# A hybrid attention trunk on one core: the opening's first loads on two queues, x's first column rounded by VectorE, and the lambda scalars moved behind the first projection pair

## The chip, the cores and the metric

The kernel runs on one core of one Trainium2 chip. The core has five engines with queues of their own: TensorE (PE in the profile, PEld for its weight loads), VectorE (DVE), ScalarE (ACT), GpSimd (POOL) and SyncE (SP), and 16 DMA engines that serve the transfers which SP, ACT and POOL issue. The metric is the device time in microseconds (us), as the median over runs.

## The reference

Two layers are applied to x, 256 tokens of 2048 features, all in float32:

```python
for l in range(2):
    h = rms_norm(x, pre_mix_norm[l])
    proj = h @ w_in[l]                     # 2048 -> 6144: q, k, v of both groups
    o_sb = stick_breaking(q_sb, k_sb, v_sb)          # 8 heads of 128
    lam = exp(sum(lq1*lk1)) - exp(sum(lq2*lk2)) + lam_init
    o_d = (softmax(q1 k1) - lam * softmax(q2 k2)) v_d  # 8 heads
    o_d = rms_norm(o_d, diff_subln) * (1 - lam_init)
    x = x + rms_norm(concat(rms_norm(o_sb), o_d) @ w_o[l], post_mix_norm[l])
    h = rms_norm(x, pre_ffn_norm[l])
    f = (silu(h @ w_gate[l]) * (h @ w_up[l])) @ w_down[l]   # 2048 -> 5632 -> 2048
    x = x + rms_norm(f, post_ffn_norm[l])
```

`lam` is one number for each layer. It comes from four vectors of 64 numbers and is used only when the second softmax is subtracted from the first. The weights are 411 MB in float32.

## The kernel before, in words

**Numbers in two parts.** A float32 product on TensorE is made of three products of rounded parts. Each weight tile `raw` (128 x 1024, two chunks of 128 rows by 512 columns) is split by ScalarE into `hi`, its rounded value (line 286), and by VectorE into `lo`, the rest (line 289). The activations are split in the same way (`xT`, lines 802 and 803). TensorE then adds hi x hi, hi x lo and lo x hi into one PSUM bank (lines 1017 to 1019).

**Stages.** In each layer come the input projection in six pairs of column blocks (`PAIRS`), the attention, which runs in pieces between the matmuls, the output projection, the gate and up projections, and the down projection. Within a pair the 2048 input rows are taken in eight steps `kp` of 256 rows. A usual step is 24 matmuls: two chunks, two token tiles, two column blocks, three products. From the second to the fifth pair, two of the eight steps (`kp` 4 and 5) are done in a form with seven block products in place of eight (a Strassen-like form, "seven"). For it VectorE and ScalarE form sums of weight tiles first (`mixed_weights`, lines 264 to 268, with `Th` and `Tl` from 259 and 260; those raw tiles are called `GU`).

**The stream of weights.** All weight tiles lie in the order of use and are fetched by SP (`fetch`, line 220), 512 KB each, into four `raw` buffers; `hi` and `lo` have six buffers each. A tile is fetched and split a few places (`LOOKAHEAD`, 4) before its use. So a fetch waits until the `lo` of the tile four places before it is done, and a `hi` waits until TensorE has finished with the tile six places before it.

**The opening** (`opening`, from line 792) is the first pair of the first layer. The activations come already transposed, as `x_columns`, two columns (128 x 2 x 256) to a transfer, into `xr`. The first weight pair is loaded in halves (line 818). Ahead of it TensorE runs `WARM` = 13 matmuls on zeros (line 367). While the opening runs, `first_stats` loads x a second time, by rows (line 853), for the first norm, and then calls `late_constants` (line 380), which loads the other gains and the rope table, and loads the lambda vectors and reduces them to the few numbers of `lamsign`, by VectorE and one exponential of ScalarE.

**Order.** A planner in the framework lays out each engine's instructions by priority (the order in which the code emits them, `high_priority` moving some ahead) with its own costs of operations. `issue_after(i)` places instructions behind `i` on the engine; `after_rests()` does so behind the last usual `lo`, `in_turn()` behind the last weight fetch. Generators (attention, flips, and with the change the lambdas) are resumed by `tick()`, which each chunk of matmuls calls; `yield 16` means sixteen ticks later. A usual step has four ticks, and so has a step of seven.

**Transfers in flight.** The transfers that SP and ACT issue share eight completion semaphores in turn, so that one waits until the transfer eight places before it has landed.

Of the kernel before, what the change touches and what calls it, by code (L numbers as in the profile page):

```python
# [9 lines left out]
F32 = mybir.dt.float32  # L10
# [3 lines left out]
ALU = mybir.AluOpType  # L14
# [6 lines left out]
L = 2  # L21
# [25 lines left out]
FORM_AT = {(0, 1): 4, (0, 2): 6, (0, 5): 5, (1, 3): 2}  # L47
DOWN_SEVEN = ((4, 7, 10, 12, 15, 17, 20), (3, 5, 8, 10, 13, 15, 18))

WARM = 13  # L50
LEVEL = 232
EARLY = 4
LEAD = 6
# [4 lines left out]
def lambda_init(layer):  # L58
    return 0.8 - 0.6 * math.exp(-0.3 * layer)
# [94 lines left out]
def kernel(  # L154
# [149 lines left out]
    def after_rests():  # L304

        return tc.issue_after(rests[-1].ins)

    def in_turn():

        return tc.issue_after(loads[-1].ins)  # L310
# [39 lines left out]
    def early_room(shape, name, dtype=F32):  # L350

        return rooms.tile(shape, dtype, tag="early", name=name)
# [14 lines left out]
        nc.tensor.matmul(spare, idle[:, 0:P], idle, start=True, stop=True)  # L367

    gains = const.tile([P, 96], F32, name="gains")
    nc.scalar.dma_start(gains[:, 0:32], gain_columns[:, 0:32])  # L370
    ident = const.tile([P, P], F32, name="ident")
    make_identity(nc, ident)
    rope_sb = const.tile([P, NT, 32], F32, name="rope_sb")
# [4 lines left out]
    lamsign = const.tile([P, L, 4], F32, name="lamsign")  # L378

    def late_constants(pool):  # L380
        lams = pool.tile([P, 4, L * 64], F32, tag="t2", name="lams")
        negones = pool.tile([P, P], F32, tag="t2", name="negones")
        nc.sync.dma_start(gains[:, 32:96], gain_columns[:, 32:96])
        nc.sync.dma_start(rope_sb, rope.rearrange("(t p) c -> p t c", p=P))
        for i, v in enumerate((lambda_q1, lambda_k1, lambda_q2, lambda_k2)):
            nc.sync.dma_start(lams[:, i, :], v.rearrange("l d -> (l d)").partition_broadcast(P))
        nc.gpsimd.memset(negones, -1.0)
        nc.vector.tensor_copy(negone, negones)
        nc.gpsimd.affine_select(
            out=negones, in_=negones, compare_op=ALU.is_ge, fill=0.0, base=0, pattern=[[-1, P]], channel_multiplier=1  # L390
        )
        nc.vector.tensor_copy(negtri, negones)
        nc.vector.tensor_copy(ident16, ident)
        nc.gpsimd.memset(hidden, NEG)
        nc.gpsimd.affine_select(
            out=hidden, in_=hidden, compare_op=ALU.is_ge, fill=0.0, base=0, pattern=[[-1, P]], channel_multiplier=1
        )
        nc.gpsimd.memset(lamsign, 1.0)
        lprod = pool.tile([P, 2, L * 64], F32, tag="t2", name="lprod")
        lsum = pool.tile([P, 2, L], F32, tag="t2", name="lsum")  # L400
        for i in range(2):
            nc.vector.tensor_tensor(out=lprod[:, i, :], in0=lams[:, 2 * i, :], in1=lams[:, 2 * i + 1, :], op=ALU.mult)
            nc.vector.tensor_reduce(
                out=lsum[:, i, :], in_=lprod[:, i, :].rearrange("p (l d) -> p l d", l=L), axis=AX.X, op=ALU.add
            )
        nc.scalar.activation(lsum, lsum, AF.Exp)
        for l in range(L):
            c0 = 80 + l * NH
            nc.vector.tensor_scalar_mul(gains[:, c0 : c0 + NH], gains[:, c0 : c0 + NH], 1.0 - lambda_init(l))
            for q in range(2):  # L410
                col = lamsign[:, l, 2 * q + 1 : 2 * q + 2]
                nc.vector.tensor_tensor(out=col, in0=lsum[:, 1, l : l + 1], in1=lsum[:, 0, l : l + 1], op=ALU.subtract)
                nc.vector.tensor_scalar_add(col, col, -lambda_init(l))

    const.tile([P, LEVEL], F32, name="level")
    eps = const.tile([P, 1], F32, name="eps")
# [374 lines left out]
    def opening(pool, accs, xT, stats, sums_of, settle):  # L791

        xr = []

        def load():
            kp = len(xr)
            xr.append(pool.tile([P, 2, S], F32, tag="tok", name=f"xr{kp}"))
            nc.sync.dma_start(xr[kp], x_columns[:, 2 * kp : 2 * kp + 2, :])

        def split(k):  # L800
            g, src = gains[:, k : k + 1], xr[k // 2][:, k % 2, :]
            nc.scalar.activation(xT[k][:, 0, :], src, AF.Copy, scale=g)
            nc.vector.scalar_tensor_tensor(
                out=xT[k][:, 1, :], in0=src, scalar=g, in1=xT[k][:, 0, :].bitcast(F32), op0=ALU.mult, op1=ALU.subtract
            )

        load()
        both = []
        for i in range(2):
            both.append((  # L810
                wpool.tile([P, 2, CW], F32, tag="raw", bufs=4, name=f"raw{i}"),
                wpool.tile([P, 2, CW], F32R, tag="hi", bufs=6, name=f"hi{i}"),
                wpool.tile([P, 2, CW], F32R, tag="lo", bufs=6, name=f"lo{i}"),
            ))
            raws.append(both[i][0])
        for kk in range(2):
            for i in range(2):
                loads.append(nc.sync.dma_start(raws[i][:, kk, :], stream[i][:, kk, :]))
        load()
        fetch(4)  # L820
        for kk in range(2):
            split(kk)
            for raw, hi, lo in both:
                nc.scalar.activation(hi[:, kk, :], raw[:, kk, :], AF.Copy)
                nc.vector.tensor_tensor(out=lo[:, kk, :], in0=raw[:, kk, :], in1=hi[:, kk, :].bitcast(F32), op=ALU.subtract)
        for i in range(2):
            ready[i] = both[i][1:]
        fed[0] = 2
        for kp in range(KT // 2):
            if kp:  # L830
                split(2 * kp)
                split(2 * kp + 1)
            if kp + 2 < KT // 2:
                load()
                fetch(2 * kp + 6)
            for part in ((0,), (1,)) if kp == KT // 2 - 1 else (range(NT),):
                eight_in(accs, xT, 0, PAIRS[0], kp, part, kp == 0, kp == KT // 2 - 1, 0)
                if kp == KT // 2 - 1:
                    settle(part[0])
            if 3 <= kp < 7:  # L840
                next(stats)
            if kp >= 4 and kp - 4 < len(IN_SEVEN):
                sums_of(IN_SEVEN[kp - 4])

    def first_stats(pool, rs):

        parts = []
        for t in range(NT):
            for h in range(0, 4, 2):
                both = early_room([P, 2, CW], f"x0_{t}_{h}")  # L850
                for j in (h, h + 1):
                    parts.append(both[:, j - h, :])
                    nc.sync.dma_start(parts[-1], xv[t][:, j * CW : (j + 1) * CW])
                if t == 1 and h == 2:
                    late_constants(pool)
                    rs += [inv_rms(u, pool, "in0", parts[4 * u : 4 * u + 4]) for u in range(NT)]
                    scales(rs)
                yield
# [23 lines left out]
    def mixer_in(pool, l, rs, xT, mix, mixed):  # L882
# [7 lines left out]
        for n, cc in enumerate(PAIRS):  # L890
# [52 lines left out]

            if n == 0 and l == 0:
                opening(pool, banks, xT, first_stats(pool, rs), sums_of, settle)
            else:
                kps = IN_ORDER if n else tuple(range(KT // 2))
                extra = None
# [428 lines left out]
```

## Time and profile before

| what | value |
|---|---|
| time before, median of 3 runs | 2197.44 us (2195.82 to 2197.62) |
| the profiled execution: its own time | 2197.66 us |
| the profiled execution: span of its instructions | 2196.0 us |
| mean granted TensorE clock | 0.998 |
| VectorE, ScalarE, GpSimd busy | 87%, 62%, 6% of the span |
| HBM read | 457.00 MB, 212 GB/s over the span with what is written |

The profiled execution is one run; its span goes from the first to the last instruction, and 1.66 us lie around it. Times in a row are counted from the span's start. A row of the timeline has the start, the duration, the engine, the line, the operation, the tile written and the tiles read, a count, and in square brackets how long the engine had been idle and what ended the idle time. Engine names with a q (SPq, ACTq) are issues of transfers. A row of the windows has for each engine the busy time and in brackets the number of instructions, then the clock, the busy share of the DMA engines and what they moved. Matmuls overlap, so that a matmul of 0.39 us starts 0.23 us after the one before it when nothing is in the way.

### The profile page before, as it was taken

What the parts mean: (1) busy time and instruction counts of PE and PEld (TensorE: products, weight loads), DVE (VectorE), ACT (ScalarE), POOL (GpSimd) and SP (SyncE); (2) the same over time, 40 slices, a digit from 0 to 9 for tenths busy, and PEclk for the clock granted to TensorE, in tenths of its full rate; (3) what the DMA queues carried; (4) which work ended last, traced back from release to release, by engine and by line L of the source; (5) the groups of instructions that cost most, each with busy time, mean ns of one, the idle gap of its engine ahead of it and who ended that gap; (6) DMA issues with size and microseconds to landing.
All of it is one profiled execution on the core that took longest, in us unless ns stands there. A gap on an engine that the chain in (4) does not pass through costs nothing.

```text
span 2196.0 us, 28541 instructions
## 1 busy us (share of the span) xinstructions
PE 2177.9 (99%) x9991; PEld 1790.8 (82%) x9991; DVE 1902.1 (87%) x2609; ACT 1370.5 (62%) x2052; POOL 138.6 (6%) x186
## 2 busy tenths in 40 slices
PE   9999999999999999999999999999999999999998
PEld 7788888788888888888878888888888888888886
DVE  7888658899999999989878886589999999999997
ACT  7566665756656656666665666657665566566664
POOL 1200000000001000000011000000000100100000
PEclk9999999999999999999999999999999999999999
DMA  9555555488687676767465455555867766767673
GB/s 308 200 170 173 192 182 172 155 279 256 196 266 243 197 251 203 244 214 262 151 251 173 160 179 189 192 170 190 276 216 244 258 216 224 241 212 234 206 266 98
DMA packets 138513, 467.28 MB, mean 213 GB/s; under 512 B 15872, under 2 KB 16640, under 8 KB 137856
## 3 DMA queue, kind: packets, MB, share of 16 engines
q1 hardware_dynamic: 122384, 436.59, 57.0%
q0 software_dynamic: 15840, 28.84, 7.5%
q8 instruction: 78, 1.28, 0.2%
q14 instruction: 67, 0.55, 0.1%
q10 hardware_dynamic: 144, 0.02, 0.0%
HBM read 457.00 MB, written 8.39 MB: 212 GB/s over the span
## 4 chain that ended last, share of the span: by engine, by line
PE 90%; DVE 4%; DMA 3%; ACT 2%; issue 1%; DVEq 0%; POOL 0%; ACTq 0%; POOLq 0%; SPq 0%
PE c L1018 9%; PE c L1019 9%; PE c L1017 9%; PE in L1017 6%; PE in L1019 6%; PE in L1018 6%; PE dn L1261 4%; PE dn L1259 4%; PE dn L1258 4%; PE p L1018 2%; PE p L1019 2%; PE p L1017 2%; PE o L528 2%; PE o L529 2%; PE o L530 2%; DMA raw<-in_weights_in_turn_dram 2%
## 5 line engine op out<-in xcount | busy, mean ns | idle before, releaser
L289 DVE TENSOR_TENSOR lo<-raw,hi 128x1024 fp32r<-128x1024 f32 x522 | 625.6, 1219 | 98.0 <-ACT hi L286 97.2
L286 ACT ACTIVATE hi<-raw 128x1024 fp32r<-128x1024 f32 x522 | 540.4, 1055 | 188.0 <-issue 51.8
L1017 PE MATMUL c<-hi,xF 128*128 128x512 f32 x834 | 328.0, 394 | 0.1
L1018 PE MATMUL c<-lo,xF 128*128 128x512 f32 x834 | 325.1, 390 | 0.7 <-DVE lo L289 0.7
L1019 PE MATMUL c<-hi,xF 128*128 128x512 f32 x834 | 324.8, 390 | 0.0
L238 POOL DMA_DIRECT2D T<-in_weights_in_turn_dram x110 | 95.9, 874 | 1684.5 <-DMA T<-in_weights_in_turn_dram 496.5
L1018 PEld LDWEIGHTS c<-lo,xF 128*128 128x128 f32 x834 | 156.7, 188 | 33.5 <-DVE lo L289 2.5
L1019 PEld LDWEIGHTS c<-hi,xF 128*128 128x128 f32 x834 | 156.5, 188 | 32.7
L1017 PEld LDWEIGHTS c<-hi,xF 128*128 128x128 f32 x834 | 156.7, 188 | 31.5 <-ACT xF L447 0.5
L1258 PE MATMUL dn<-hi,jh 128*128 128x512 f32 x432 | 168.3, 389 | 0.0
L1259 PE MATMUL dn<-lo,jh 128*128 128x512 f32 x432 | 168.1, 389 | 0.0
L289 DVE TENSOR_TENSOR lo<-G,hi 128x1024 fp32r<-128x1024 f32 x110 | 133.9, 1218 | 29.8 <-ACT hi L286 29.6
L259 ACT ACTIVATE hi<-T 128x1024 fp32r<-128x1024 f32 x110 | 115.5, 1050 | 45.6 <-PE c L1019 31.3
L259 ACT ACTIVATE Th<-G 128x1024 fp32r<-128x1024 f32 x110 | 116.1, 1055 | 37.9 <-DVE G L268 35.9
L260 DVE TENSOR_TENSOR Tl<-G,Th 128x1024 fp32r<-128x1024 f32 x110 | 133.9, 1217 | 5.3 <-ACT Th L259 5.3
L260 DVE TENSOR_TENSOR lo<-T,hi 128x1024 fp32r<-128x1024 f32 x110 | 133.9, 1217 | 4.3 <-ACT hi L259 4.0
L268 DVE TENSOR_TENSOR G<-G,T 128x1024 f32<-128x1024 f32 x110 | 134.2, 1220 | 2.1
L259 ACT ACTIVATE Th<-T 128x512 fp32r<-128x512 f32 x110 | 68.9, 627 | 104.6 <-DVE T L267 88.7
L1261 PE MATMUL dn<-hi,jl 128*128 128x512 f32 x432 | 132.9, 390 | 0.0
L1017 PE MATMUL in<-hi,xT 128*128 128x512 f32 x328 | 131.3, 401 | 0.0
L1017 PE MATMUL in<-hi,xI 128*128 128x512 f32 x328 | 131.1, 401 | 0.0
L1018 PE MATMUL in<-lo,xT 128*128 128x512 f32 x328 | 128.2, 391 | 0.4 <-DVE lo L289 0.4
(448 smaller groups left out, 4736.8 us busy)
## 6 DMA issues: line engine op xcount, KB each, us to landing
raw<-in_weights_in_turn_dram SPq DMA_DIRECT2D x522, 512.0 KB, 4.5
T<-in_weights_in_turn_dram SPq DMA_DIRECT2D x110, 512.0 KB, 6.3
G<-in_weights_in_turn_dram SPq DMA_DIRECT2D x110, 512.0 KB, 5.8
T<-in_weights_in_turn_dram POOLq DMA_DIRECT2D x110, 256.0 KB, 7.1
GU<-in_weights_in_turn_dram SPq DMA_DIRECT2D x32, 512.0 KB, 6.2
V<-in_weights_in_turn_dram SPq DMA_DIRECT2D x8, 512.0 KB, 4.1
away_ffn<-x SPq DMA_DIRECT2D x8, 512.0 KB, 8.4
xd<-away_ffn SPq DMA_DIRECT2D x8, 512.0 KB, 8.4
```

The source lines that it names most:

```text
L238: nc.gpsimd.dma_start(sums[i][:, 0, :], stream[i - 1][:, 0, :], accum_op=ALU.add)
L259: nc.scalar.activation(h, w, AF.Copy)
L260: nc.vector.tensor_tensor(out=l, in0=w, in1=h.bitcast(F32), op=ALU.subtract)
L268: nc.vector.tensor_tensor(out=g, in0=g, in1=t2.unsqueeze(1).to_broadcast([P, 2, CW]), op=ALU.add)
L286: nc.scalar.activation(hi, raw, AF.Copy)
L289: rest = nc.vector.tensor_tensor(out=lo, in0=raw, in1=hi.bitcast(F32), op=ALU.subtract)
L1017: nc.tensor.matmul(a, sh, hi, start=first, stop=False, skip_group_check=open_sums[0])
L1018: nc.tensor.matmul(a, sh, lo, start=False, stop=False, skip_group_check=open_sums[0])
L1019: nc.tensor.matmul(a, sl, hi, start=False, stop=last, skip_group_check=open_sums[0])
L1258: nc.tensor.matmul(accs[c, t], sh, hi[:, kk, :], start=first, stop=False, skip_group_check=open_sums[0])
L1259: nc.tensor.matmul(accs[c, t], sh, lo[:, kk, :], start=False, stop=False, skip_group_check=open_sums[0])
L1261: nc.tensor.matmul(accs[c, t], sl, hi[:, kk, :], start=False, stop=last, skip_group_check=open_sums[0])
```

## The change

It has four parts.

1. `WARM` is 10 and not 13.
2. The opening's first loads: the first two columns of x and the gains that go with them are issued by ACT, the columns one by one (128 KB each); SP starts with the weights. The first column is rounded by VectorE (`opened`, with high priority) and no longer by ScalarE, and the four `lo` of the first weight pair are placed behind that instruction.
3. The other 64 columns of the gains are loaded by GpSimd and no longer by SP.
4. The lambdas leave `late_constants` and become a generator that is started behind the opening. Its four loads are placed behind the last weight fetch emitted by then, its arithmetic sixteen ticks later, behind the last usual `lo`. Its tile comes from the four `early` buffers, which held x for the first norm.

```diff
-WARM = 13
+WARM = 10
...
     gains = const.tile([P, 96], F32, name="gains")
-    nc.scalar.dma_start(gains[:, 0:32], gain_columns[:, 0:32])
...
     def late_constants(pool):
-        lams = pool.tile([P, 4, L * 64], F32, tag="t2", name="lams")
         negones = pool.tile([P, P], F32, tag="t2", name="negones")
-        nc.sync.dma_start(gains[:, 32:96], gain_columns[:, 32:96])
+        nc.gpsimd.dma_start(gains[:, 32:96], gain_columns[:, 32:96])
         nc.sync.dma_start(rope_sb, rope.rearrange("(t p) c -> p t c", p=P))
-        for i, v in enumerate((lambda_q1, lambda_k1, lambda_q2, lambda_k2)):
-            nc.sync.dma_start(lams[:, i, :], v.rearrange("l d -> (l d)").partition_broadcast(P))
...
-        lprod = pool.tile([P, 2, L * 64], F32, tag="t2", name="lprod")
-        lsum = pool.tile([P, 2, L], F32, tag="t2", name="lsum")
+
+    def lambdas():
+
+        room = early_room([P, 2 * CW], "lams")
+        lams = room[:, 0 : 4 * L * 64].rearrange("p (i c) -> p i c", i=4)
+        lprod = room[:, 4 * L * 64 : 6 * L * 64].rearrange("p (i c) -> p i c", i=2)
+        lsum = room[:, 6 * L * 64 : 6 * L * 64 + 2 * L].rearrange("p (i l) -> p i l", i=2)
+        with in_turn():
+            for i, v in enumerate((lambda_q1, lambda_k1, lambda_q2, lambda_k2)):
+                nc.sync.dma_start(lams[:, i, :], v.rearrange("l d -> (l d)").partition_broadcast(P))
+        yield 16
         for i in range(2):
-            nc.vector.tensor_tensor(out=lprod[:, i, :], in0=lams[:, 2 * i, :], in1=lams[:, 2 * i + 1, :], op=ALU.mult)
+            with after_rests():
+                nc.vector.tensor_tensor(out=lprod[:, i, :], in0=lams[:, 2 * i, :], in1=lams[:, 2 * i + 1, :], op=ALU.mult)
             nc.vector.tensor_reduce(
                 out=lsum[:, i, :], in_=lprod[:, i, :].rearrange("p (l d) -> p l d", l=L), axis=AX.X, op=ALU.add
             )
         nc.scalar.activation(lsum, lsum, AF.Exp)
         for l in range(L):
             c0 = 80 + l * NH
-            nc.vector.tensor_scalar_mul(gains[:, c0 : c0 + NH], gains[:, c0 : c0 + NH], 1.0 - lambda_init(l))
+            with after_rests():
+                nc.vector.tensor_scalar_mul(gains[:, c0 : c0 + NH], gains[:, c0 : c0 + NH], 1.0 - lambda_init(l))
             for q in range(2):
                 col = lamsign[:, l, 2 * q + 1 : 2 * q + 2]
                 nc.vector.tensor_tensor(out=col, in0=lsum[:, 1, l : l + 1], in1=lsum[:, 0, l : l + 1], op=ALU.subtract)
                 nc.vector.tensor_scalar_add(col, col, -lambda_init(l))
+        yield
...
+        opened = []
+
         def split(k):
             g, src = gains[:, k : k + 1], xr[k // 2][:, k % 2, :]
-            nc.scalar.activation(xT[k][:, 0, :], src, AF.Copy, scale=g)
+            if k == 0:
+                with tc.high_priority(offset=URGENT):
+                    opened.append(nc.vector.tensor_scalar(out=xT[k][:, 0, :], in0=src, scalar1=g, scalar2=None, op0=ALU.mult))
+            else:
+                nc.scalar.activation(xT[k][:, 0, :], src, AF.Copy, scale=g)
...
-        load()
+        xr.append(pool.tile([P, 2, S], F32, tag="tok", name="xr0"))
+        nc.scalar.dma_start(gains[:, 0:32], gain_columns[:, 0:32])
+        nc.scalar.dma_start(xr[0][:, 0, :], x_columns[:, 0, :])
+        nc.scalar.dma_start(xr[0][:, 1, :], x_columns[:, 1, :])
...
             for raw, hi, lo in both:
                 nc.scalar.activation(hi[:, kk, :], raw[:, kk, :], AF.Copy)
-                nc.vector.tensor_tensor(out=lo[:, kk, :], in0=raw[:, kk, :], in1=hi[:, kk, :].bitcast(F32), op=ALU.subtract)
+                with tc.issue_after(opened[0].ins):
+                    nc.vector.tensor_tensor(out=lo[:, kk, :], in0=raw[:, kk, :], in1=hi[:, kk, :].bitcast(F32), op=ALU.subtract)
...
                 opening(pool, banks, xT, first_stats(pool, rs), sums_of, settle)
+                start(lambdas())
```

## Prediction

> **What bounds the kernel now.** I read the page's busy shares first.
>
> ```profile
> PE 2177.9 (99%) x9991; PEld 1790.8 (82%) x9991; DVE 1902.1 (87%) x2609; ACT 1370.5 (62%) x2052; POOL 138.6 (6%) x186
> ```
>
> TensorE is the bound: it is busy for 2177.9 of 2196.0 us. The change adds or takes no product, so only the 18 us in which TensorE has no matmul can shrink or grow, and of these only the ones near the change. The next view gives the busy time by stretches.
>
> ```profile
> 0.00:14.00 14.00, 12.37 (x40) 6.82 (x41) 6.35 (x12) 7.89 (x13) 1.17 (x10) 1.00 0.86 285
> 14.00:60.00 46.00, 46.00 (x203) 37.80 (x202) 36.47 (x74) 33.17 (x58) 10.33 (x15) 1.00 0.93 322
> 60.00:80.00 20.00, 18.68 (x83) 14.88 (x81) 18.74 (x20) 12.39 (x14) 3.77 (x4) 1.00 0.55 194
> 80.00:300.00 220.00, 220.00 (x1088) 180.02 (x1087) 163.47 (x264) 137.79 (x260) 8.87 (x16) 1.00 0.54 181
> ```
>
> The first busy time in each row is TensorE's. It has holes in the first 14 us and between 60 and 80 us, none from 14 to 60 and none from 80 to 300 us. The change touches just the stretch up to about 90 us. The timelines of the engines show the two holes from near.
>
> ```profile
> 6.71 0.51 PE L1017 MATMUL in<-hi,xT 128*128 128x512 f32 x1
> ...
> 12.47 0.39 PE L1019 MATMUL in<-hi,xT 128*128 128x512 f32 x1
> 12.70 0.39 PE L1017 MATMUL in<-hi,xT 128*128 128x512 f32 x1
> 13.45 0.50 PE L1018 MATMUL in<-lo,xT 128*128 128x512 f32 x1 [0.37 <-DVE lo L289]
> ...
> 64.37 0.39 PE L1019 MATMUL q_in<-hi,slin 128*128 128x512 f32 x1
> 66.08 0.50 PE L1017 MATMUL p_in<-Th,shin 128*128 128x512 f32 x1 [1.31 <-ACT Th L259]
> ```
>
> The pitch of matmuls is 12.70 - 12.47 = 0.23 us. So the first hole behind the start is 13.45 - 12.70 - 0.23 = 0.52 us, and the second is 66.08 - 64.37 - 0.23 = 1.48 us. Before 6.71 us no product can run.
>
> **Part 1, the opening's loads.** These rows carry it: the issues of ACT and SP, the warm-up, the landing of the first x (from the chain), and the first work on weights.
>
> ```profile
> 0.84 0.39 ACTq L370 DMA_DIRECT2D gains<-in_gain_columns_dram  x1
> 5.62 0.63 ACT L824 ACTIVATE hi<-raw 128x512 fp32r<-128x512 f32 x1 [3.53 <-DMA raw<-in_weights_in_turn_dram]
> ```
> ```profile
> 1.25 0.42 SPq L818 DMA_DIRECT2D raw<-in_weights_in_turn_dram  x1
> ```
> ```profile
> 1.26 5.68 PE L367 MATMUL spare<-idle 128*128 128x512 bf16 x13 [1.26 <-DVE idle L364]
> ```
> ```profile
> 6.89 0.48 DVE L803 SCALAR_TENSOR_TENSOR xT<-xr,gains,xT 128x256 fp32r<-128x256 f32 x1
> ```
> ```profile
> 0.81 4.09 DMA xr<-in_x_columns_dram
> ```
>
> x takes 4.09 us from its issue at 0.81 to its landing, the first weight half 5.62 - 1.25 = 4.37 us. In the changed kernel SP's first issue is the weight half, so it lands at 0.81 + 4.09 to 4.37 = 4.9 to 5.2 us, and ScalarE's `hi` (0.63) ends at 5.5 to 5.8. ACT issues x's first column behind the gains, at 0.84 + 0.39 = 1.23 or a little later; it lands at 5.3 to 5.6, and VectorE rounds it in 0.48 us at most (I take the duration of its three-operand operation on the same shape): 5.8 to 6.1. The two roundings now run side by side, where ScalarE did them in turn. So the first product starts 0.6 to 0.9 us earlier. The four `lo` are queued behind the rounding on VectorE, but the first of them needs the `hi` that ends at about the same time, so that wait costs nothing. The two more issues of ACT (0.4 us each) end by 2.1 us, in front of 3 us in which ACT waits anyway.
>
> What is late next? The 25th product needs the `hi` and the 26th the `lo` of the third weight tile.
>
> ```profile
> 11.08 1.06 ACT L286 ACTIVATE hi<-raw 128x1024 fp32r<-128x1024 f32 x1 [0.40 <-DMA raw<-in_weights_in_turn_dram]
> ```
> ```profile
> 12.18 1.22 DVE L289 TENSOR_TENSOR lo<-raw,hi 128x1024 fp32r<-128x1024 f32 x1 [0.83 <-ACT hi L286]
> ```
> ```profile
> 2.50:3.00 0.50, 0.50 (x3) 0.20 (x2) 0.00 (x0) 0.00 (x0) 0.00 (x0) 1.00 1.00 206
> ```
>
> The tile lands at 11.08; `hi` and `lo` follow without a gap, and the 26th product starts at 13.45. From there to 64.60 TensorE has no hole. So the start of the 26th product alone sets the time, and what is won before it becomes a longer wait in front of it: 0.52 + 0.6 to 0.9 us. It moves only if the landing at 11.08 moves. In front of it lie the same bytes as before (two columns of x, four weight halves, two more columns, 2 MB with the tile itself), and the DMA engines are full (share 1.00 in the last row), so I put it at nothing. Bounds: a gain of 0.9 us if the landing follows SP's earlier start, a loss of 0.5 us, because the columns come in smaller pieces, and even as it is the early traffic moves only 206 GB/s, against a mean of 322 from 14 to 60 us.
>
> The three matmuls fewer in the warm-up take 3 x 5.68 / 13 = 1.3 us, and it ends at about 5.6 instead of 6.9 us, in front of the first product at 5.8 to 6.1. No price, apart from the clock, which is a rival below.
>
> **Part 2, the loads of the lambdas and gains leave SP.** SP's issues before the second pair:
>
> ```profile
> 34.16 0.33 SPq L383 DMA_DIRECT2D gains<-in_gain_columns_dram  x1
> 34.97 0.38 SPq L384 DMA_DIRECT2D rope_sb<-in_rope_dram  x1
> 36.23 0.34 SPq L386 DMA_DIRECT2D lams<-in_lambda_q_dram  x1
> ...
> 38.89 0.33 SPq L386 DMA_DIRECT2D lams<-in_lambda_k_dram  x1
> 39.62 0.33 SPq L220 DMA_DIRECT2D raw<-in_weights_in_turn_dram  x1
> ```
> ```profile
> 32.81 6.74 DMA x<-in_x_dram
> ```
> ```profile
> 40.00:42.00 2.00, 2.00 (x11) 1.65 (x10) 1.44 (x7) 1.78 (x7) 0.29 (x1) 1.00 0.22 33
> ```
>
> Each issue waits until the one eight places before has landed: the weight fetch of 39.62 waits for the x that was issued at 32.81. Six tiny transfers (the gains, the rope table, four lambda loads) hold six of the eight places, and from 40 to 42 us the DMA engines carry 33 GB/s. Without the gains and the four lambda loads, rope takes the place at 34.16 and the first weight fetch of the second pair that at 34.97, 39.62 - 34.97 = 4.65 us earlier, if its buffer is free by then. The second can have the place at 36.23; those behind need buffers that come free only with the opening's last tiles, and I give them about 1 us. The lambda loads go behind the fetches of the second pair's first tiles, where SP has nothing to issue.
>
> What that is worth shows in ACT's rows.
>
> ```profile
> 47.32 0.21 ACT L406 ACTIVATE lsum<-lsum 128x4 f32<-128x4 f32 x1 [4.92 <-DVE lsum L403]
> 47.98 1.06 ACT L286 ACTIVATE hi<-raw 128x1024 fp32r<-128x1024 f32 x1 [0.46 <-DMA raw<-in_weights_in_turn_dram]
> ...
> 53.12 1.07 ACT L286 ACTIVATE hi<-raw 128x1024 fp32r<-128x1024 f32 x1
> 54.07 1.07 ACT L286 ACTIVATE hi<-GU 128x1024 fp32r<-128x1024 f32 x1
> 57.66 1.06 ACT L259 ACTIVATE hi<-GU 128x1024 fp32r<-128x1024 f32 x1 [2.52 <-DVE GU L264]
> ```
>
> ScalarE stands for 4.92 us at the lambdas' exponential, then starts the second pair's first `hi` at 47.98, when its tile lands, and has five `hi` and four settling copies (of the opening's results) until the mixed tile at 57.66. From there it is 66.08 - 57.66 = 8.4 us to the product that waits for `Th`. In the changed kernel the first two `hi` can be done before 47.98; the next two must wait until TensorE is through with earlier tiles. At the least, the last usual `hi` (53.12) is done before the settling copies, and the one of 54.07 moves up to 53.12; with its `lo` and the sum behind it, each no longer waiting for the one before, the mixed tile starts about 1.2 us earlier. At the most, the `hi` of 54.07 goes ahead of the last settling copies too, which end at about 53.1 after two of 0.6 us; it then starts near 51, and the mixed tile about 3 us earlier. The hole is 1.48 us. I take 1.4 of it as gone: nearer to the whole, since the larger shift covers it twice and the smaller leaves 0.3 us. Bounds: 0 and 1.48.
>
> **Part 3, the lambdas' arithmetic, later.**
>
> ```profile
> 86.81 1.23 DVE L289 TENSOR_TENSOR lo<-raw,hi 128x1024 fp32r<-128x1024 f32 x1 [3.24 <-ACT hi L286]
> ```
> ```profile
> 46.67 0.29 DVE L402 TENSOR_TENSOR lprod<-lams 128x128 f32<-128x128 f32 x1 [2.90 <-DMA lams<-in_lambda_k_dram]
> ```
>
> It is four operations of 0.29 us and ten of about 0.15 us or less, some of them overlapping, 2.1 us in all. Sixteen ticks are four steps, so they are emitted when the second seven starts, behind the `lo` of the tiles fed by then; I place them at 78 to 83 us. VectorE is busy for 18.74 of the 20 us from 60 to 80, and stands idle for 3.24 us up to 86.81. That idle time covers the 2.1 us: no price. Without the cover it is up to 2.1 us and the wait for the exponential. The results are first used in the differential heads' weights, behind transposes that come later still.
>
> The gains by GpSimd: that engine is busy for 6% of the span, and the columns are first used with the lambdas. No price; bounds 0 and 0.2 us, for 32 KB among the opening's traffic at 206 GB/s if the planner issues it that early.
>
> **The sum.** 0 (opening) - 1.4 (hole at 64.6) + 0 (lambdas) = -1.4 us. Against the profiled execution's own 2197.66 that is 2196.3; the median of the runs lies 0.2 us below that execution, so I predict 2196.0 us. That is 0.06%; what a measurement of this kernel can tell from no change I take as 0.2%, 4.4 us.
>
> **Rivals.**
> - *The opening carries through*: the third tile lands up to 0.9 us earlier, since two queues start filling the engines together. For it speaks the slow early traffic, against it the full engines. With part 2: 2197.4 - 1.4 - 0.8 = 2195.2.
> - *The hole stays*: the planner keeps the mixed tile's chain behind the settling copies and other `lo`, and TensorE, not the fetch, paces the splits. For it: the third and fourth `hi` gain little. 2197.4.
> - *The lambdas land in the chain of the second seven*, the other side. VectorE is full there. If the planner puts the arithmetic before that seven's last `Tl`, TensorE waits 2.1 us, and VectorE also stands for the exponential, 2.1 + 0.2 us if that is queued behind two `hi`. The rows in point are these; the `Tl` ends at 77.78, 0.05 us before its product:
>
> ```profile
> 76.56 1.22 DVE L260 TENSOR_TENSOR Tl<-GU,Th 128x1024 fp32r<-128x1024 f32 x1
> ```
> ```profile
> 77.83 0.50 PE L1018 MATMUL p_in<-Tl,shin 128*128 128x512 f32 x1
> ```
>   That gives 2197.4 + 2.1 = 2199.5 with the gain of part 2 lost in the same queue, and with the exponential's wait 2201.8. It decides if any lambda operation stands ahead of that `Tl`.
> - *The clock*: warm-up matmuls start every 5.68 / 13 = 0.44 us, later ones every 0.23. With a shorter warm-up the slow pitch could last longer, at 0.21 us for each product. The wait of 1.1 to 1.4 us in front of the 26th swallows the first five or six; all 25 would leave 4 us, 2200; I take eight, a third, which leave 0.3 us, 2196.3. The Trainium skill, TensorE: Matmul & The Clock Gate, Part 1, says the full clock comes after a busy window of about 3.4 us that runs free of the kernel's start; by that rule 3.4 us more at the slow pitch are eight products, an estimate, and the sum would be 2196.3 instead of 2196.0. The trace agrees that the pitch halves (0.44 and 0.23); when it would with ten matmuls no run here shows.
>
> **How the numbers follow.** My forecast 0.46, the opening carries through 0.12, the hole stays 0.16, the lambdas in the way 0.18, the clock 0.05, something else 0.03. All but the third rival lie within 0.2%. Of the third, the half with the exponential's wait, 0.09, is slower by more; with 0.03 for the unnamed that is 0.12. No case reaches faster by 0.2%; I take 0.04 for it from the forecast and the first rival, in case parts 1 and 2 are worth more than the rows let me see. The rest, 0.84, is no change. The range is from 2195.2 less 0.8 for the spread of the runs, 2194.4, to 2200.0, which takes in the third rival without the exponential; the forecast's own is 2195.0 to 2197.0.
>
> **What would show it.** Right: first product at 5.8 to 6.1 us, a wait of over 1 us before the 26th, which starts within 0.5 us of 13.45; a weight fetch at about 35 us; no 4.92 us stand of ScalarE; the hole at 64.6 under 0.3 us; lambda operations after the last `Tl` of the second seven, and 1.4 us less at every later mark. Wrong: the 26th product earlier than 12.9 or later than 14; a hole before the first or second seven of over 1 us; or a difference that first shows after 100 us, where nothing is changed.

## The result, and the profile after

The changed kernel takes 2191.14 us (median of 8 runs, 2190.34 to 2191.68). The kernel before, run beside it, takes 2197.78 us (8 runs, 2195.82 to 2200.58). The ratio is 0.997, with a 95% interval of 0.9961 to 0.9979. The change is worth 6.6 us, or 0.3%. The prediction was 2196.0 us, with a range down to 2194.4. So the forecast of 1.4 us, too little to tell from no change, was wrong: the gain is real, and nearly five times the forecast.

The profiled execution of the changed kernel took 2191.05 us, with a span of 2189.4 us. TensorE is still the bound, as the page's busy shares show:

```profile
PE 2174.9 (99%) x9988; PEld 1791.1 (82%) x9988; DVE 1901.3 (87%) x2610; ACT 1370.9 (63%) x2051; POOL 139.1 (6%) x187
```

I set every VectorE instruction of one trace against the same instruction of the other. The changed kernel is 0 to 0.6 us ahead from 13 to 45 us and 1.47 us ahead from 100 to 375 us. That is almost the forecast (1.4). It is still 1.54 us ahead at 400 us. Then, between 420 and 457 us, it gains 4.6 us more and is 6.15 us ahead. Two further steps of 0.2 us follow at about 1540 us and at 2166 us. So nearly all of the miss has one place. It lies at the gate and up projections of the first layer, where the change touches nothing. The prediction had named this as a sign of its being wrong ("a difference that first shows after 100 us").

The busy times by stretches show the opening, the first sevens and that place; the first busy time in a row is TensorE's, and the column before the DMA share is the granted clock. The changed kernel:

```profile
0.00:14.00 14.00, 12.20 (x36) 7.59 (x37) 6.85 (x13) 7.99 (x13) 1.95 (x11) 1.00 0.78 272
...
60.00:80.00 20.00, 20.00 (x91) 16.28 (x90) 18.21 (x23) 11.35 (x14) 0.69 (x1) 1.00 0.57 193
...
410.00:460.00 50.00, 50.00 (x229) 41.42 (x228) 47.81 (x81) 32.32 (x49) 4.36 (x5) 1.00 0.78 260
434.00:436.00 2.00, 2.00 (x10) 1.65 (x10) 2.00 (x3) 0.71 (x1) 0.00 (x0) 1.00 0.97 387
```

The same view of the kernel before, at the place that was not forecast:

```profile
410.00:460.00 50.00, 47.78 (x211) 38.82 (x210) 43.40 (x78) 31.15 (x48) 3.80 (x5) 0.97 0.71 239
434.00:436.00 2.00, 2.00 (x7) 1.51 (x6) 2.00 (x5) 0.87 (x2) 0.00 (x0) 0.50 0.00 0
```

From 60 to 80 us TensorE's hole is gone (18.68 before, 20.00 now). From 410 to 460 us it had 2.22 us of holes before the change and has none now. From 434 to 436 us the clock was at one half before the change and is whole now.

What happens there starts at GpSimd. In the gate and up stage GpSimd adds a second half tile onto each tile `T` while transferring it (line 238). It waits until SP's transfer of `T` has landed and then issues its own. GpSimd's timeline before the change:

```profile
417.23 1.93 POOL L238 DMA_DIRECT2D T<-in_weights_in_turn_dram  x2 [265.20 <-PE c L1019]
```

and after it:

```profile
411.09 0.89 POOL L238 DMA_DIRECT2D T<-in_weights_in_turn_dram  x1 [260.52 <-PE c L1037]
413.24 0.86 POOL L238 DMA_DIRECT2D T<-in_weights_in_turn_dram  x1 [1.27 <-DVE rsq_ffn L433]
```

The bracket gives a wrong picture here, since it names a product as the releaser. The trace's semaphore records say more. The products are not what it waited for: their semaphore had been raised 258 times by 412.41 us, and with 258 five of the kernels below have already started the same transfer. Before the change, `T` landed at 412.27 us and GpSimd's wait passed at 412.30, but the transfer started only at 417.23, 4.93 us later. In the changed kernel the wait passes at 410.53 and the transfer starts at 411.09, 0.56 us later. So the two accumulations landed at 423.00 and 426.71 us before, and land at 418.37 and 419.65 now. What followed before the change shows in the timeline of ScalarE,

```profile
426.87 1.06 ACT L259 ACTIVATE hi<-T 128x1024 fp32r<-128x1024 f32 x1 [1.79 <-DMA T<-in_weights_in_turn_dram]
```

and, through the chain of the mixed tile, in that of TensorE:

```profile
429.73 0.39 PE L1019 MATMUL q<-hi,sl 128*128 128x512 f32 x1
431.45 0.50 PE L1017 MATMUL p<-Th,sh 128*128 128x512 f32 x1 [1.33 <-ACT Th L259]
432.84 0.50 PE L1018 MATMUL p<-Tl,sh 128*128 128x512 f32 x1 [0.88 <-DVE Tl L260]
```

With a pitch of 0.23 us the holes are 431.45 - 429.73 - 0.23 = 1.49 and 432.84 - 431.45 - 0.23 = 1.16 us, 2.65 us together. Behind them the clock was at half from 433.43 to 436.84 us, which costs half of 3.41 us, 1.7 us. Together that is 4.35 us of the 4.6. In the changed kernel ScalarE takes up the second `T` at 421.38 without a wait, and TensorE has no hole.

### The profile page after: what moved, and what is told of

Same layout as the page of the kernel before. It is cut to its first block, busy times and chain, and to the rows that moved or that the text cites. A ratio compares the mean times of both kernels' runs of the same rounds, so it can differ in the third digit from the quotient of the medians.

```text
span 2189.4 us, 28540 instructions
## 1 busy us (share of the span) xinstructions
PE 2174.9 (99%) x9988; PEld 1791.1 (82%) x9988; DVE 1901.3 (87%) x2610; ACT 1370.9 (63%) x2051; POOL 139.1 (6%) x187
## 4 chain that ended last, share of the span: by engine, by line
PE 95%; DVE 3%; ACT 1%; DMA 0%; issue 0%; DVEq 0%; SPq 0%; ACTq 0%
PE c L1037 10%; PE c L1038 10%; PE c L1036 10%; PE in L1036 7%; PE in L1038 7%; PE in L1037 7%; PE dn L1280 4%; PE dn L1278 4%; PE dn L1277 4%; PE p L1037 3%; PE p L1038 2%; PE p L1036 2%; PE o L536 2%; PE o L537 2%; PE o L538 2%; PE dn L1037 1%
## 5 line engine op out<-in xcount | busy, mean ns | idle before, releaser
L1036 PE MATMUL in<-hi,xT 128*128 128x512 f32 x328 | 131.9, 404 | 0.5 <-ACT hi L841 0.5
L1038 PE MATMUL in<-hi,xT 128*128 128x512 f32 x328 | 128.4, 392 | 0.0
```

What stands on the lines that cost most here:

```text
L1036: nc.tensor.matmul(a, sh, hi, start=first, stop=False, skip_group_check=open_sums[0])
L1038: nc.tensor.matmul(a, sl, hi, start=False, stop=last, skip_group_check=open_sums[0])
```

## The experiments

All experiments compute the whole result. Ratios are to the kernel before, with 95% intervals. Fences show rows of the run that they follow.

**First theory: GpSimd's first transfer of a program starts late.** Before the change the accumulation at 412 us was GpSimd's first transfer of all; now it is that of the gains, at 1.41 us. Four kernels tell this apart from other causes. The first adds a tiny transfer early, into a tile that nobody reads:

```diff
         nc.gpsimd.memset(lamsign, 1.0)
+        nc.gpsimd.dma_start(level[:, 0:16], gain_columns[:, 0:16])
```

> The kernel before with one small transfer by GpSimd added near the start (16 gain columns, 8 KB, into a tile that nobody reads); the order of every other instruction on every engine stays as it was, and the gains stay on SP. Theory (GpSimd's first transfer of a program starts about 4.4 us late, and before that was the accumulation of the first gate tile at 412 us): 4.4 to 5.0 us less than before, 2192.8 to 2193.4, GpSimd's accumulation within 0.7 us of its wait, no half clock at 433 us. Rival 1 (the earlier weight fetches, or other timing of the changed kernel, shortened the stage at 412 us): as before, 2197.8. Rival 2 (the place in GpSimd's instruction stream decides): 2193 here too, and then the kernel with memsets tells it apart.

The second puts it at 152 us, behind the eighth rotation:

```diff
         eng.tensor_tensor(out=v16, in0=ra, in1=rb, op=ALU.add)
+        turned.append(nm)
+        if len(turned) == 8:
+            eng.tensor_copy(level[:, 0:16], tok[:, 0:16])
+            eng.dma_start(level[:, 0:16], gain_columns[:, 0:16])
```

> The kernel before with the same small transfer by GpSimd, but behind the last rotation of layer 0, at about 152 us, where nothing waits for GpSimd for 260 us. Theory: the transfer stands 4.4 to 4.9 us behind GpSimd's last operation before it is issued, the accumulation at 412 us then starts within 0.7 us of its wait, and the time is 2192.8 to 2193.4. If the late start is a matter of GpSimd having been idle for 260 us, it is paid again at 412 us, and the time stays at 2197.8. Rival 1 (timing): 2197.8.

The third adds instructions and no transfer:

```diff
-        nc.gpsimd.memset(lamsign, 1.0)
+        for _ in range(4):
+            nc.gpsimd.memset(lamsign, 1.0)
```

> The kernel before with three more memsets by GpSimd near the start and no transfer. Theory: as before, 2197.8, with the 4.9 us stand at 412 us. Rival 2 (place in GpSimd's instruction stream): the stand is gone or changed, down to 2193. Rival 1: 2197.8.

The fourth takes the gains' transfer by GpSimd out of the changed kernel:

```diff
-        nc.gpsimd.dma_start(gains[:, 32:96], gain_columns[:, 32:96])
+        nc.sync.dma_start(gains[:, 32:96], gain_columns[:, 32:96])
```

> The changed kernel with the later gains loaded by SP again, so that GpSimd's first transfer is the accumulation at about 411 us. Theory: the stand of about 4.9 us and the stretch at half clock are back, 4.4 to 5.0 us more than the changed kernel, 2195.5 to 2196.2, and up to 0.5 us more for the place on SP's queue. Rival 1 (the gain at 412 us comes from the earlier fetches): 2191.1 to 2191.6. Rival 2: 2191 to 2196, by where the stream comes to lie.

Measured: 2193.59 us with the early transfer (0.9974, 0.9964 to 0.9984), 2193.86 with the late one (0.9978, 0.9969 to 0.9988), 2193.70 with the three memsets (0.9976, 0.9967 to 0.9985), and 2191.25 with the gains back on SP (0.9965, 0.9952 to 0.9977). The first two fit the theory in time. But the late first transfer does not stand: GpSimd's copy ends at 151.98 us, and the transfer follows in its timeline after 0.33 us:

```profile
152.30 0.74 POOL L794 DMA_DIRECT2D level<-in_gain_columns_dram  x1 [0.33 <-POOL level L793]
```

The memsets, which hold no transfer at all, bring the same 4 us, and the changed kernel without the early transfer keeps its time. The theory that a first transfer is late by itself has fallen.

**Second theory: the border of an instruction block.** The transfers that carry instructions (queue q14 in the view of the DMA queues, 8 KB a packet) gave the next lead. That view of the kernel before, from 412 to 417 us (packets, MB, share of the DMA engines):

```profile
q1 hardware_dynamic: 531, 1.92, 94.8%
q14 instruction: 1, 0.01, 0.4%
```

The packet starts at 415.33 us, inside the 4.93 us stand. No such packet moves in that stretch in the changed kernel, nor in the four kernels above; each of them has one at 148.4 to 150.1 us instead, where the kernel before has none. The block is GpSimd's, since it moves with the count of GpSimd's instructions alone. The kernel before has 67 GpSimd rows in the trace ahead of the wait at 412 us; the five others have 68 to 70. So a block's border lies near this wait: with 68 rows or more ahead of the wait the packet comes long before it, with 67 only 3.03 us behind it. The theory is that GpSimd then stands for the block. Four more kernels move this border by giving memsets to VectorE and change the order of nothing else. Two are the changed kernel with two and with one memset fewer on GpSimd:

```diff
-    nc.gpsimd.memset(eps, EPS)
+    nc.vector.memset(eps, EPS)
-        nc.gpsimd.memset(lamsign, 1.0)
+        nc.vector.memset(lamsign, 1.0)
```

> The changed kernel with two of GpSimd's memsets (of eps and lamsign) given to VectorE, so that GpSimd has as many instructions ahead of its first accumulation as before the change (67 rows of the trace up to that wait); the gains' transfer by GpSimd stays. New theory (GpSimd's instructions are fetched in blocks of 8 KB, and in the kernel before a block begins just behind the wait at 412.30 us, is asked for only when the wait passes, and costs 4.9 us): the stand is back with an instruction fetch inside it, and so are the holes and the half clock; 4.4 to 5.0 us more than the changed kernel, 2195.5 to 2196.2. Rival (GpSimd's first transfer): no stand, since the first transfer is at 1.4 us as before; 2191.2. Rival (a chance meeting with other transfers at 412 us, which any shift of times undoes): 2191.2.

> The changed kernel with one memset (of eps) given to VectorE: GpSimd has one instruction more ahead of the wait than before the change. New theory: the block is asked for by the time the wait itself is read, at about 149 us, while GpSimd stands in front of it; no stand, 2191.2. Rivals: 2191.2 as well; the run shows that the memset on VectorE by itself costs nothing.

(the second with the `eps` line alone), and two the kernel before with one (`eps`) and three (`eps`, `lamsign`, `hidden`) fewer:

> The kernel before with the memset of eps given to VectorE: one GpSimd instruction fewer than before. New theory: the block then begins behind the first accumulation's issue; the first accumulation starts within 0.7 us of its wait, the second stands for 4 to 5 us with an instruction fetch inside; T's second landing is as late as before, the first is not; between 1 and 4.6 us of loss against a kernel without the stand, 2194.2 to 2198. Rival (first transfer): stand before the first accumulation as before, 2198. Rival (chance meeting): about 2193.5.

> The kernel before with three memsets (eps, lamsign, hidden) given to VectorE: three GpSimd instructions fewer. New theory: the block begins behind the second accumulation, is asked for at about 414 us and is needed only at 441 us; no stand, although GpSimd's first transfer is still that accumulation and no instruction was added; 2193.0 to 2194.0, as with the three memsets more. Rival (first transfer): the stand stays, 2198. Rival (chance meeting): 2193.5.

Measured: 2191.29 us with two fewer in the changed kernel (0.9966, 0.9954 to 0.9979), 2191.36 with one (0.9964, 0.9951 to 0.9978), 2193.72 with one fewer in the kernel before (0.9976, 0.9967 to 0.9986), 2193.42 with three (0.9975, 0.9965 to 0.9985). The block moved as the theory says (413.12 us with 67 rows, 147.71 with 68, 415.51 with 66, 418.66 with 64), but the time did not follow: the changed kernel with two fewer was expected to lose 4.4 to 5.0 us and the kernel before with one fewer at least 1 us, and neither lost any. The changed kernel with 67 rows has the fetch behind the wait, which passed at 409.25 us, and no stand; GpSimd's timeline:

```profile
410.17 0.89 POOL L238 DMA_DIRECT2D T<-in_weights_in_turn_dram  x1 [260.83 <-PE c L1037]
412.50 0.86 POOL L238 DMA_DIRECT2D T<-in_weights_in_turn_dram  x1 [1.44 <-DMA T<-in_weights_in_turn_dram]
```

So the border alone has fallen too. What is left is that both are needed.

**Third theory: first transfer and block border together.** Two kernels bring both together and one keeps the border alone. The first is the changed kernel with the gains on SP and `eps` on VectorE (67 rows, first transfer at the wait); the second is the kernel before with `eps` on VectorE and one memset of `lamsign` more, so that other instructions make up the same count; the third is the kernel with the early tiny transfer and `eps` on VectorE (67 rows, not the first transfer).

> The changed kernel with both: the later gains on SP, so that GpSimd's first transfer is the accumulation at about 410 us, and the memset of eps on VectorE, so that 67 rows of GpSimd lie ahead of its wait. Theory now (the stand needs two things together: GpSimd's first transfer of the program, and the border of an instruction block right behind the wait in front of it): the stand of 4 to 5 us is back, with a fetch inside it, and the time is 2195.4 to 2196.4. Rival (the stand hangs on how the transfers at 412 us meet, which the earlier fetches of the changed kernel move): no stand, 2191.3.

> The kernel before with the memset of eps on VectorE and one memset of lamsign more on GpSimd: as many GpSimd rows as before, its first transfer still the accumulation, the order on the other engines as it was but for one memset of VectorE. Theory (first transfer and block border together): the stand stays, 2197.4 to 2198.4. Rival (how the transfers meet): the times at 412 us hardly move, so the stand stays too, 2197.4 to 2198.4. If it is gone (2193.5), both fall, and what is left is something of the program's layout that a count of instructions does not catch.

> The kernel before with the small transfer by GpSimd at the start and the memset of eps on VectorE: 67 GpSimd rows ahead of the wait as before, and the accumulation is no longer the first transfer. Theory (both together): no stand, the accumulation starts within 1 us of its wait, the fetch comes after the wait (at 412 to 416 us) and nothing stands for it; 2193.0 to 2194.0. If the block border alone makes the stand: 2197.8.

Measured: 2195.85 us (0.9993, 0.9984 to 1.0001), 2197.06 (1.0000, 0.9991 to 1.0009) and 2193.02 (0.9981, 0.9972 to 0.9989). The stand is back in the changed kernel, in GpSimd's timeline

```profile
414.69 1.93 POOL L238 DMA_DIRECT2D T<-in_weights_in_turn_dram  x2 [265.05 <-PE c L1038]
```

after a wait that passed at 409.76 us. It is there in the second (411.33 to 416.09 us; the time lies 0.3 us below what was expected), and gone in the third, whose wait passed at 411.92:

```profile
412.84 1.80 POOL L238 DMA_DIRECT2D T<-in_weights_in_turn_dram  x2 [261.12 <-DVE lo L289]
```

Over all 16 traces the time from GpSimd's wait to its first accumulation falls into four cells:

| GpSimd rows ahead of the wait | the accumulation is GpSimd's first transfer | another came before |
|---|---|---|
| 67 | 4.93, 4.93, 4.76 us (before; changed with gains on SP and `eps` moved; before with `eps` swapped) | 0.92, 0.92 us |
| 64, 66, 68 to 70 | 0.65 us (five traces) | 0.56 us (six traces) |

Against 0.56 us each alone costs 0.1 to 0.4 us, and both together 4.2 to 4.4 us. In all three stands the block's packet starts 2.9 to 3.1 us after the wait passes (3.03, 3.05, 2.94), and GpSimd goes on 1.8 to 1.9 us after that. In the two kernels with 67 rows and no stand the packet starts only after both accumulations (413.12 us behind 410.17 and 412.50; 415.20 behind 412.84 and 413.75), so there the accumulations do not need that block. That GpSimd stands for the block in the other three is therefore not shown. What it does in the meantime, and why the pair is needed, these traces do not show; it stays open. In time the stand costs 2195.85 - 2191.25 = 4.6 us in the changed kernel, and 2197.06 less 2193.02 to 2193.86 in the kernel before, 3.2 to 4.0 us.

In the traces the price differs with the clock. I set TensorE's products of each kernel against those of the kernel before, from 410 to 470 us. The 13 kernels without the stand gain 4.1 to 4.4 us on it; the two others with the stand gain 0.94 and 1.23 us, so that theirs costs about 3.5 and 3.2 us. The kernel before shows the half clock behind its two holes; the profiles of the two others show a whole clock, and holes of 1.47 and 1.16, and of 1.13 and 1.16 us. These are TensorE's rows of the first of them, the changed kernel with 67 rows and the gains on SP:

```profile
427.24 0.39 PE L1038 MATMUL q<-hi,sl 128*128 128x512 f32 x1
428.94 0.50 PE L1036 MATMUL p<-Th,sh 128*128 128x512 f32 x1 [1.31 <-ACT Th L259]
430.32 0.50 PE L1037 MATMUL p<-Tl,sh 128*128 128x512 f32 x1 [0.88 <-DVE Tl L260]
```

How often the clock falls to half in the runs without a profile is not on record, so the medians' 4.6 against 3.2 to 4.0 us can't be put down to it.

Full clock came at 6.76 us in the trace of before, and 433.43 - 6.76 = 426.67 us is 125 times 3.413 us, the length of the slow stretch; in the 15 other traces the one stretch at full clock is 637, 638 or 639 times as long. So the clock is decided in windows of 3.413 us. In that trace both holes (1.49 and 1.16 us, from 429.96 on) fall but for 0.05 us into the window from 430.01 to 433.43. In the other two, whose full clock came at 6.03 and 6.78 us, a border lies between them (429.28 and 430.03 us, 124 windows later), and no window has more than 1.6 us of hole. The Trainium skill, TensorE: Matmul & The Clock Gate, Part 1, says that the window is 3413 ns long and runs free of the kernel; the traces agree. The Trainium skill, same page, Why this matters for your kernels, says to avoid gaps of over about 3 us; here two gaps of 1.49 and 1.16 us in one window were enough.

**The other 2.4 us: opening and lambdas.** The six forms of the kernel before without the stand lie at 2193.0 to 2193.9 us (I take 2193.6), the changed one at 2191.1 to 2191.4 in its forms without it. One kernel is the changed one with the opening and the thirteen warm-up matmuls as before; one is the kernel before with the changed opening alone, and a memset more against the stand; one is the changed kernel with `WARM = 13`.

> The changed kernel with the opening and its thirteen warm-up matmuls as before the change: only the lambdas' loads and arithmetic and the gains by GpSimd are changed. My step for part 2 gives 1.4 us less than a kernel before without the stand (2193.6): 2192.2. If the opening is worth nothing, as forecast, the whole changed kernel's 2191.2 is reached but for the spread: 2191.2 to 2192.2. If the opening is worth the rest, 2192.2 or more.

> The kernel before with the changed opening alone (loads on two queues, x's first column rounded by VectorE, ten warm-up matmuls) and one memset of GpSimd more, so that the stand at 412 us is absent. My step for part 1 (worth nothing): as the kernels before without the stand, 2193.0 to 2193.9. The rival of the prediction (the opening carries through, 0.7 to 0.9 us): 2192.1 to 2193.1, with the third weight tile at hand by 10.4 us and the 26th product by 13.1.

> The changed kernel with thirteen warm-up matmuls instead of ten; GpSimd's instructions as in the changed kernel. If the shorter warm-up costs (the changed kernel's profile has the full clock only from 10.33 us, other profiles with ten from 4.8 to 6.0): 2190.5 to 2191.0. If the window in which the clock comes falls by chance, and ten are enough: 2191.0 to 2191.6. If the warm-up then ends behind the first weights and stands in the way of the first product: up to 2191.8.

Measured: the lambdas alone 2192.64 us (0.9980, 0.9972 to 0.9989), the opening alone 2192.83 (0.9977, 0.9967 to 0.9987), thirteen warm-up matmuls 2191.13 (0.9968, 0.9957 to 0.9980). Against 2193.6 the one part is worth about 1.0 us, the other 0.8, and both together 2.4. The 2.4 holds for five forms against six. How it splits is an estimate from medians: the intervals of the two kernels reach about 2 us to either side, and the runs of the lambdas alone go from 2191.33 to 2196.07. The opening alone is early at the third tile and at the 26th product; ScalarE's and TensorE's rows of that kernel:

```profile
9.28 1.06 ACT L286 ACTIVATE hi<-raw 128x1024 fp32r<-128x1024 f32 x1 [0.36 <-DMA raw<-in_weights_in_turn_dram]
```

```profile
12.33 0.39 PE L1028 MATMUL in<-lo,xT 128*128 128x512 f32 x1
...
52.03 0.50 PE L1028 MATMUL in<-lo,xT 128*128 128x512 f32 x1 [0.76 <-DVE lo L289]
...
65.65 0.73 PE L1027 MATMUL p_in<-Th,shin 128*128 128x512 f32 x2 [1.33 <-ACT Th L259]
```

The 26th product is 1.1 us earlier than before, but at 65 us only 0.4 is left (65.65 against 66.08): a wait of 0.76 us at 52 us, which the kernel before does not have, takes the rest back, and the wait at 65 us is as long as before. In the changed kernel both waits are gone. This would make the two parts worth more together, but the medians are too close to show it. The shorter warm-up makes no difference: 2191.13 with thirteen, 2191.14 with ten.

## Why the prediction was wrong, point by point

**The gains by GpSimd ("No price; bounds 0 and 0.2 us"): the step that failed.** It was priced as 32 KB of traffic. What it did was to make the accumulation at 412 us no longer GpSimd's first transfer, and to add one instruction ahead of it; the change as a whole also put one more wait there (69 rows instead of 67). Either alone removes the stand: with the transfer and 67 rows there is none (changed kernel with two memsets fewer), nor with 68 rows and no earlier transfer (gains back on SP). The rows for it were in the profile of before, at a place that I never looked at because "the change touches just the stretch up to about 90 us": the row of 417.23 us, and 2.22 us of holes between 410 and 460 us in a kernel with 18 in all. The hole could have been read there, though not that the change would remove it. That it did was luck: nothing in the change was aimed at it, and 4.4 of the 6.6 us hang on which transfer of GpSimd comes first and on how many instructions stand ahead of it.

**Part 1, the opening (0; bounds -0.9 and +0.5).** Wrong in its middle, inside its bounds. The first product came at 6.25 us instead of 5.8 to 6.1, since VectorE could take up x's first column only at 5.75 us and not at 5.3 to 5.6, and the 26th at 13.94, 0.49 us later than before; TensorE's timeline of the changed kernel:

```profile
6.25 1.62 PE L1036 MATMUL in<-hi,xT 128*128 128x512 f32 x3 [0.54 <-ACT hi L841]
...
13.71 0.39 PE L1036 MATMUL in<-hi,xT 128*128 128x512 f32 x1
13.94 0.39 PE L1037 MATMUL in<-lo,xT 128*128 128x512 f32 x1
```

There was no wait of over 1 us before the 26th, because the products before it ran at the slow pitch until the full clock at 10.33 us. In this one execution the clock rival came true. But this execution is the exception: in the other five profiles with ten warm-up matmuls the full clock came at 4.75 to 6.91 us, and in the ten with thirteen at 3.93 to 7.10. The window that decides runs free, and 10.33 is one window of 3.41 us later than 6.92. Why this execution missed that window stays open: the opening alone had nearly the same hole behind its warm-up (0.51 against 0.54 us) and the full clock at 6.91 us. Over the seven profiles with the changed opening ScalarE starts on the third tile at 9.28 to 10.72 us (mean 10.06), over the nine with the old one at 9.97 to 11.90 (mean 11.10). The 26th product follows at a mean of 12.69 against 13.50. So up to the 26th product the rival "the opening carries through" (0.8 us) is what happens on average. What failed is "In front of it lie the same bytes as before ... I put it at nothing": the third tile is taken up 1.0 us earlier on average. The single landing of 11.08 on which the sum stood was one draw from a spread of nearly 2 us.

**Part 2, the loads off SP's queue (-1.4; bounds 0 and -1.48).** Right in mechanism and nearly in size. The weight fetch starts at 34.10 us (forecast 35), the lambda loads follow behind the second pair's first tiles; SP's rows:

```profile
34.10 6.71 SPq L220 DMA_DIRECT2D raw<-in_weights_in_turn_dram  x4
40.86 0.93 SPq L220 DMA_DIRECT2D GU<-in_weights_in_turn_dram  x2
41.84 0.43 SPq L404 DMA_DIRECT2D lams<-in_lambda_q_dram  x1
```

ScalarE has no stand of 4.92 us; it takes up the tiles at 42.12 us and makes `Th` at 61.81, and the product that waited for it follows without a hole in TensorE's rows:

```profile
42.12 1.99 ACT L286 ACTIVATE hi<-raw 128x1024 fp32r<-128x1024 f32 x2
...
61.81 1.07 ACT L259 ACTIVATE Th<-GU 128x1024 fp32r<-128x1024 f32 x1 [2.03 <-DVE GU L268]
```

```profile
64.48 0.39 PE L1038 MATMUL q_in<-hi,slin 128*128 128x512 f32 x1
64.71 0.39 PE L1036 MATMUL p_in<-Th,shin 128*128 128x512 f32 x1
```

The mixed tile's chain starts on ScalarE at 55.79 us, 1.87 us earlier than before (forecast 1.2 to 3). The hole of 1.48 us is gone, 1.37 us at that product. The term was still a little large: in seven of the eight other traces with the old queue the wait for `Th` is 0.9 us, not the 1.3 of the execution from which it was taken. The medians' 1.0 us fits this, but is not clear of the spread. "The hole stays" fell.

**Part 3, the lambdas' arithmetic (0).** Right. It runs behind the second seven's last `Tl`, in VectorE's idle time, which shrinks from 3.24 to 1.75 us; its timeline:

```profile
74.01 1.23 DVE L260 TENSOR_TENSOR Tl<-GU,Th 128x1024 fp32r<-128x1024 f32 x1 [0.53 <-ACT Th L259]
...
77.43 0.48 DVE L408 TENSOR_TENSOR lams<-lams 128x128 f32<-128x128 f32 x2
...
85.38 2.36 DVE L289 TENSOR_TENSOR lo<-raw,hi 128x1024 fp32r<-128x1024 f32 x2 [1.75 <-ACT hi L286]
```

The rival on the other side, the lambdas ahead of that `Tl`, did not come.

**The sum.** -1.4 was forecast. Measured between medians: the stand 3.2 to 4.6, and 2.4 for the opening and the lambdas' loads together, which split into 0.8, 1.0 and 0.6 for the two together only as an estimate. The small differences at about 1540 us and at the end were not followed up; against the kernel before, five other kernels lose 1.1 to 1.6 us at 1520 to 1560 us with no edit there.

## What to carry to other kernels

Look at the whole timeline for holes of the bounding engine before saying which stretch a change can touch: an added instruction can move an instruction block's border, and a first transfer can move from a critical place to a free one. Where GpSimd's first transfer lies on a critical path, give it an idle one at the start; it costs nothing here (early transfer: 2193.59 against 2197.8) and takes the place of luck in the count of instructions. And do not put a term of 1 us on one landing of one profile: take its spread from several executions, or carry it in the range.

## What the runs showed of the hardware that I had not expected

- GpSimd's instructions come in 8 KB packets, and the request for one waits behind a semaphore wait in front of it: it moves at 147.7 to 150.5 us with 68 rows or more, and only after the wait at 409 to 412 us with 67 or fewer. The Trainium skill, Runtime: NRT & Kernel Launch, Instruction fetch mechanics, says that the next block is fetched while the current one runs, so that crossing costs little. The four traces with the packet behind the wait and no stand agree (0.65 to 0.92 us from wait to transfer). The three in which it met GpSimd's first transfer took 4.76 to 4.93 us; that the fetch itself is what takes so long is not shown.
- A granted clock of one half for 3.41 us after two holes of 1.49 and 1.16 us, when both fell into one window; holes of 1.47 and 1.16, and of 1.13 and 1.16 us, on two sides of a border left the clock whole.
- The moment of the full clock at the start is between 3.93 and 7.10 us in 15 of 16 traces and 10.33 in one, with ten or thirteen warm-up matmuls alike.
